# Attention stage: low parts of weights by subtraction on VectorE, or by an adding transfer from memory with the weights sent one ahead

## The chip, the cores and the metric

The kernel runs on one core of a Trainium2 chip. TensorE (PE) multiplies; VectorE (DVE) and ScalarE (ACT) do elementwise work; GpSimd (POOL) and SyncE (SP) mostly issue transfers (DMAs), each from a queue of its own that it works off in order. What counts is the device time of one execution in microseconds (us), the median of the runs.

## The reference

Two layers over 512 frames of width 1024, with 256 memory tokens. Layer 0 mixes by an RWKV-7 recurrence; layer 1, which the change touches, by attention to chunks. In short form:

```python
k_s, v_s = split(rms_norm(x, ln_kv) @ w_kv, 2)            # 12 heads of 64
h = rms_norm(x, ln1[1]);  p = h @ b_w_in                  # 768 mixer + 256 memory columns
s = q . k / 8 + rel_bias                                  # own chunk of 64 and 8 chunks before
mix = softmax(s) @ v
mo  = memory_attention(p[768:], mem_n, w_mem_kv[1])       # 4 heads, 256 memory tokens
x = x + concat([mix, mo]) @ w_out[1]
x = x + conv_glu(rms_norm(x, ln2[1]), ffn_in[1], ...)     # then a last rms_norm
```

All is float32.

## The kernel before, in words

**Three products for one.** A float32 matrix product is made of three products in a faster format (fp32r). Each operand is split into a high part (the value rounded to the format) and a low part (what is left), and PE adds high·high, high·low and low·high. `r1h`/`r1l` and `r2h`/`r2l` are the parts of the two normalised activations (`r1` for keys and values, `r2` for queries); `whi` and `wlo` are those of a weight of 128 x 1024 numbers, 512 KB.

**A weight's way to PE.** `load_w` has SP send the raw weight into `wraw` (L180; 2 buffers). `split_w` has ACT round it to `whi` (L169). Then the low part is made in one of two ways. By subtraction: DVE computes `wlo = wraw - whi` (L175). By an adding transfer: ACT writes the rounded negative, `wlo = -wraw` (L172), and POOL's queue sends the same weight from memory again, added onto it (L173). `whi` and `wlo` have 3 buffers each, so the low part of a weight can only be begun when PE is done with the low part of the third weight before it. The switch `lo_on` chooses; in the kernel before it is on only in layer 0's mixing stage.

**`dense`** multiplies one weight: 16 matmuls with the high part (L198, L199), then 8 with the low part (L202), each 512 columns wide. Its results lie in a PSUM tile `psd`, of which there are two.

**The attention stage** (from 782 us of the profiled execution) has 22 such weights: 6 for queries and 2 for memory queries (`wB`, `q_proj`), 6 for keys (`w_kvk`, `k_proj`), 3 times 2 for values (`w_kvv`, `v_proj`), and 2 of the output projection (`w_out`, `out_ahead`). `v_proj` makes a group of values, 256 columns, for 512 frames in four quarters; in a quarter each of 8 steps has three matmuls, two high (L1032, L1033) and one low (L1034), 256 wide; ACT then moves the quarter out (L1036, `vS`). The stage opens with `run(chain(*qk(0), v_proj(0)))`: q0, k0, then the first values. Then `weave` (L82) takes turns, by costs written beside each `yield`, between six pairs of attention heads with the memory attention (scores L1053/L1054, DVE L1058, exponentials on ACT L1060, DVE L1062, transposes L1068, copies on ACT L1070, products with values L1082) and the other projections. `attention` also loads the bias tiles `big` on SP (L1043) and has POOL write a corner of each (L1044).

A scheduler then fixes the order of every engine's instructions at build time; each engine works its own list off in order, so an instruction that waits holds up all that stands behind it on its engine.

Of the kernel before, what the change touches and what calls it, by code (L numbers as in the profile page):

```python
# [111 lines left out]
def trunk_kernel(ctx, tc, A, out):  # L112
# [25 lines left out]
    def Vc(name, i):  # L138
        return vec[:, VOFF[name][0] + i:VOFF[name][0] + i + 1]

    def ps_d(shape=(P, S)):
        return banks["D"].tile(list(shape), F32, name="psd", tag="psd")
# [17 lines left out]
    def tmp(dt=F32, shape=(P, S)):  # L160
        return banks["tmp"].tile(list(shape), dt, name="tmp", tag="tmp")


    lo_on = [0]

    def split_w(raw, n, src=None):
        hi = wp.tile([P, 1024], F32R, name="whi", tag="whi")
        lo = wp.tile([P, 1024], F32R, name="wlo", tag="wlo")
        SC.copy(hi[:, :n], raw)  # L169
        if src is not None:  # L170

            SC.activation(lo[:, :n], raw, AF.Copy, scale=-1.0)  # L172
            GP.dma_start(lo[:, :n], src, accum_op=ALU.add)  # L173
        else:
            V.tensor_tensor(lo[:, :n], raw, hi[:, :n], op=ALU.subtract)  # L175
        return hi, lo

    def load_w(src, n=1024):
        raw = wp.tile([P, 1024], F32, name="wraw", tag="wraw", bufs=2)
        nc.sync.dma_start(raw[:, :n], src)  # L180
        return split_w(raw[:, :n], n, src if lo_on[0] else None)
# [8 lines left out]
    def dense(ps, units, act, order=None, start=True, stop=True):  # L190

        ks = [(w, j, k) for w, kk in units for j, k in enumerate(kk)]
        if order is not None:
            ks = [next(q for q in ks if q[2] == k) for k in order]

        for n, ((wh, wl), j, k) in enumerate(ks):
            ah, al = act(k)
            PE.matmul(ps, wh[:, j * P:(j + 1) * P], ah, start=start and n == 0, stop=False)  # L198
            PE.matmul(ps, wh[:, j * P:(j + 1) * P], al, start=False, stop=False)  # L199
            yield 432  # L200
        for n, ((wh, wl), j, k) in enumerate(ks):
            PE.matmul(ps, wl[:, j * P:(j + 1) * P], act(k)[0], start=False, stop=stop and n == len(ks) - 1)  # L202
            if n % 2 or n == len(ks) - 1:
                yield 432 if n % 2 else 216
# [5 lines left out]
    def pair_of(h_, l_):  # L210
        return lambda k: (h_[:, k], l_[:, k])
# [25 lines left out]
    def scaled_split(src, m, gain, h_, l_):  # L237
        SC.activation(h_[:, m], src, AF.Copy, scale=Vc(gain, m))
        V.scalar_tensor_tensor(l_[:, m], src, Vc(gain, m), h_[:, m], op0=ALU.mult, op1=ALU.subtract)
# [73 lines left out]
        return 2 * (2 * (2 * score + 2 * 430) + 1720)  # L313


    def out_ahead(l, act, order, n, pre):

        for m in range(n):
            w = load_w(A["w_out"][l, m])
            ps = ps_d()  # L320
            pre.append((w, ps))
            yield from dense(ps[:], [(w, K8)], act, order=order, stop=False)
# [572 lines left out]
    pre = []  # L895
    lo_on[0] = 1
    for st_ in range(NPAIR + 1):
# [28 lines left out]
        if st_ == NPAIR:  # L926
            if NM < 18:
                gens.append((mA, mem_cost(860) * (18 - NM) / 18))
            gens.append((out_ahead(0, act1, [0, 1, 2, 3, 4] if NM < 18 else [0, 1, 2, 3, 6, 7, 4], 2, pre), (10 if NM < 18 else 14) * 648))
# [10 lines left out]
    act2 = pair_of(r2h, r2l)  # L940
# [11 lines left out]
    with ExitStack() as bctx:  # L952
# [15 lines left out]
        def take_back(*ms):  # L968
            for m in ms:
                yield lambda: (m if m < 4 else f"m{m - 6}") in done  # L970
                t_ = tmp()
                nc.sync.dma_start(t_[:], mixb[m])
                split_to(r2h[:, m], r2l[:, m], t_[:])
                yield 1

        for m in range(KD):
            scaled_split(xT[:, m], m, "ln_kv", r1h, r1l)


        done = set()  # L980
# [3 lines left out]
        def after_unit(i, n):  # L984
            at = UNITS.index(i) - n
            return lambda: at < 0 or UNITS[at] in done

        def q_proj(i, T, unit=None):
            yield after_unit(i if unit is None else unit, 3)
            w = load_w(A["wB"][i])  # L990
            ps = ps_d()
            yield from dense(ps[:], [(w, K8)], act2)
            q = tmp()
            V.scalar_tensor_tensor(q[:], ps[:], 0.125, rho[:], op0=ALU.mult, op1=ALU.mult)

            qs = ap_.tile([P, 2, S], F32R, name="qs", tag="qs", bufs=3)
            for h in range(2):
                SC.copy(qs[HS[h], h], q[HS[h]])
                V.tensor_tensor(qs[HS[1 - h], h], q[HS[h]], qs[HS[h], h], op=ALU.subtract)
            T["q"] = qs  # L1000

        def k_proj(i, T):
            yield after_unit(i, 2)
            w = load_w(A["w_kvk"][i])
            ps = ps_d()
            yield from dense(ps[:], [(w, K8)], act1)
            k_ = tmp()
            V.tensor_tensor(k_[:], ps[:], rho[:], op=ALU.mult)
            ks = ap_.tile([P, 2, S], F32R, name="ks", tag="ks")
            kl = ap_.tile([P, 2, S], F32R, name="kl", tag="kl")  # L1010
            for h in range(2):
                SC.copy(ks[HS[h], h], k_[HS[h]])
                SC.copy(ks[HS[1 - h], h], k_[HS[h]])
                for rows_ in HS:
                    V.tensor_tensor(kl[rows_, h], k_[HS[h]], ks[HS[h], h], op=ALU.subtract)
            T["k"] = ks, kl
# [3 lines left out]
        def v_proj(g):  # L1020
            yield lambda: g < 2 or 2 * g - 3 in done
            vS[g] = ap_.tile([P, 4, 256], F32, name="vS", tag="vS")
            wv = [load_w(A["w_kvv"][g, u]) for u in range(2)]
            for t2 in range(2):
                pp_ = ps_d()
                for t in (2 * t2, 2 * t2 + 1):
                    pt = pp_[:, (t % 2) * 256:(t % 2) * 256 + 256]
                    ts = slice(t * P, (t + 1) * P)
                    for k in range(8):
                        wh, wl = wv[k // 4]  # L1030
                        ws = slice((k % 4) * 256, (k % 4 + 1) * 256)
                        PE.matmul(pt, r1h[:, k, ts], wh[:, ws], start=k == 0, stop=False)  # L1032
                        PE.matmul(pt, r1l[:, k, ts], wh[:, ws], start=False, stop=False)  # L1033
                        PE.matmul(pt, r1h[:, k, ts], wl[:, ws], start=False, stop=k == 7)  # L1034
                        yield 324
                    SC.activation(vS[g][:, t], pt, AF.Copy, scale=rc[:, t:t + 1])  # L1036

        def attention(i, T):
# [54 lines left out]

        Tb = [{} for _ in range(NPAIR)]
        qk = lambda i: [q_proj(i, Tb[i]), k_proj(i, Tb[i])]
        run(chain(*qk(0), v_proj(0)))
        ptB = {}

# [7 lines left out]
        def mem_qk(f):  # L1106
            yield from q_proj(6 + f, Tm[f], f"m{f}")
            yield after_unit(f"m{f}", 2)
            ks = ap_.tile([P, 2, S], F32R, name="ks", tag="ks")
            kl = ap_.tile([P, 2, S], F32R, name="kl", tag="kl")  # L1110
            for h in range(2):
                SC.copy(ks[HS[h], h, :NMEM], kmT1[HS[h], f])
                SC.copy(ks[HS[1 - h], h, :NMEM], kmT1[HS[h], f])
                for rows_ in HS:
                    V.tensor_tensor(kl[rows_, h, :NMEM], kmT1[HS[h], f], ks[HS[h], h, :NMEM], op=ALU.subtract)
            Tm[f]["k"] = ks, kl
# [10 lines left out]
        def wait_for(c):  # L1127
# [4 lines left out]
        pre = []  # L1132
        att = [attention(i, Tb[i]) for i in range(NPAIR)]
        weave([(chain(*att[:2], wait_for(lambda: "k" in Tm[1]), memB, *att[2:]), NPAIR * ATT_COST + mem_cost(430)),
               (chain(*qk(1), mem_qk(0), mem_qk(1), v_proj(1), *qk(2), *qk(3), v_proj(2), q_proj(4, Tb[4]),
                      q_proj(5, Tb[5]), k_proj(4, Tb[4]), take_back(0, 1, 2, 6, 7), k_proj(5, Tb[5]), take_back(3),
                      out_ahead(1, act2, [0, 1, 2, 6, 7, 3], 2, pre)),
                1.05 * (6 * 16 * 648 + 2 * 32 * 324 + 12 * 648))])

    with ExitStack() as fctx:  # L1140
        open_banks(fctx, S=2, F=4)
# [123 lines left out]
```

## Time and profile before

| | |
|---|---|
| median of 3 runs | 1388.37 us (1387.73 to 1388.55) |
| profiled execution | 1385.81 us, of which 1384.0 us from the first to the last instruction |
| busy in it | PE 96%, DVE 60%, ACT 44%, POOL 2% |
| attention stage | about 782 to 976 us; output projection to 1012; channel mixer to the end |

Rows of the profile read as follows. A group or timeline row names the line, the engine, the operation and "out<-in" tiles; an arrow "<-" in brackets, or at a row's end, names what ended the idle time before the instruction. A waits row says who waited, at which line, for which engine and line, for how long in total, how many times, and the longest.

### The profile page before, as it was taken

To read this page: it belongs to the slowest core of one execution; us is meant where nothing else is said; L and a number is where in the kernel's file an instruction comes from. 1 tells how busy PE (TensorE), PEld (TensorE's weight loads), DVE (VectorE), ACT (ScalarE), POOL (GpSimd) and SP (SyncE) were. 2 spreads that over 40 slices of the span, in tenths; PEclk is the share of its full clock that TensorE was granted. 3 is DMA by queue.
4 is the path that set the end of the run, shared out by engine and by line. 5 is a ranking of instruction groups with operands and counts; after the bars stand their busy time and mean duration, and the time that the engine had idled before them with its cause. 6 is when DMAs were issued, how large, how long until landed. Compare 5 with 4: busy or idle time off the path is not lost. (4 is left out here: it accounts for less than half of the span.)

```text
span 1384.0 us, 20864 instructions
## 1 busy us (share of the span) xinstructions
PE 1331.9 (96%) x8266; PEld 1075.5 (78%) x8266; DVE 826.1 (60%) x1752; ACT 612.7 (44%) x1022; POOL 33.7 (2%) x55
## 2 busy tenths in 40 slices
PE   6999999998899999999999999999999999999996
PEld 4877777775678888888888887787788888888886
DVE  7876789776356565655343567658566555553324
ACT  6556556544344333333232466657443333332321
POOL 3000000000000000000000000000000000000000
PEclk9999999998789999999999999999999999999998
DMA  5275544460042223233233331233222322322332
GB/s 180 87 214 128 110 108 106 94 159 24 1 152 92 91 94 104 92 99 95 73 110 98 124 107 65 93 106 99 92 92 91 105 94 93 106 88 82 104 95 74
DMA packets 63506, 139.18 MB, mean 101 GB/s; under 512 B 24624, under 2 KB 28336, under 8 KB 63408
## 3 DMA queue, kind: packets, MB, share of 16 engines
q1 hardware_dynamic: 60672, 127.89, 29.4%
q0 software_dynamic: 2736, 9.96, 4.3%
q8 instruction: 65, 1.06, 0.3%
q14 instruction: 33, 0.27, 0.1%
HBM read 131.01 MB, written 6.82 MB: 100 GB/s over the span
## 5 line engine op out<-in xcount | busy, mean ns | idle before, releaser
L175 DVE TENSOR_TENSOR wlo<-wraw,whi 128x1024 fp32r<-128x1024 f32 x183 | 218.9, 1197 | 130.1 <-PE psd L202 119.9
L169 ACT CAST whi<-wraw 128x1024 fp32r<-128x1024 f32 (+1 forms) x202 | 207.8, 1030 | 156.5 <-DMA wraw<-in_ffn_out_dram 40.5
L198 PE MATMUL psd<-r1h,whi 128*128 128x512 f32 x336 | 138.9, 414 | 5.4 <-ACT r1h L214 3.8
L198 PE MATMUL psf<-r1h,whi 128*128 128x512 f32 x352 | 137.2, 390 | 0.0
L198 PE MATMUL psf<-r2h,whi 128*128 128x512 f32 x352 | 137.1, 390 | 0.0
L199 PE MATMUL psf<-r1l,whi 128*128 128x512 f32 x352 | 137.0, 389 | 0.0
L199 PE MATMUL psf<-r2l,whi 128*128 128x512 f32 x352 | 137.0, 389 | 0.0
L199 PE MATMUL psd<-r1l,whi 128*128 128x512 f32 x336 | 135.1, 402 | 0.0
L202 PE MATMUL psd<-r1h,wlo 128*128 128x512 f32 x336 | 95.5, 411 | 3.1 <-DMA wlo<-in_wA_dram 3.1
L199 PE MATMUL psd<-f3l,whi 128*128 128x512 f32 (+1 forms) x238 | 88.6, 377 | 0.0
L198 PE MATMUL psd<-f3h,whi 128*128 128x512 f32 (+1 forms) x238 | 88.5, 376 | 0.0
L202 PE MATMUL psf<-r1h,wlo 128*128 128x512 f32 x352 | 87.0, 389 | 0.0
L202 PE MATMUL psf<-r2h,wlo 128*128 128x512 f32 x352 | 86.9, 389 | 0.0
L358 DVE TENSOR_TENSOR tmp<-psf,rho 128x512 f32<-128x512 f32 x44 | 30.4, 692 | 94.7 <-PE psf L202 94.7
L198 PEld LDWEIGHTS psd<-r1h,whi 128*128 128x128 f32 x336 | 64.4, 192 | 22.0 <-ACT r1h L214 4.2
L198 PE MATMUL psd<-r2h,whi 128*128 128x512 f32 (+1 forms) x200 | 77.5, 391 | 0.1
L199 PE MATMUL psd<-r2l,whi 128*128 128x512 f32 (+1 forms) x200 | 76.3, 384 | 0.8 <-DVE r2l L215 0.8
L202 PEld LDWEIGHTS psf<-r1h,wlo 128*128 128x128 f32 x352 | 66.1, 188 | 13.7
L202 PEld LDWEIGHTS psf<-r2h,wlo 128*128 128x128 f32 x352 | 66.1, 188 | 13.7
L198 PEld LDWEIGHTS psf<-r1h,whi 128*128 128x128 f32 x352 | 66.1, 188 | 13.7
L199 PEld LDWEIGHTS psf<-r1l,whi 128*128 128x128 f32 x352 | 66.1, 188 | 13.7
L198 PEld LDWEIGHTS psf<-r2h,whi 128*128 128x128 f32 x352 | 66.1, 188 | 13.7
(324 smaller groups left out, 2433.1 us busy)
## 6 DMA issues: line engine op xcount, KB each, us to landing
wraw<-in_ffn_in_dram SPq DMA_DIRECT2D x88, 512.0 KB, 3.3
wraw<-in_ffn_out_dram SPq DMA_DIRECT2D x32, 448.0 KB, 3.3
wraw<-in_wA_dram SPq DMA_DIRECT2D x20, 512.0 KB, 3.9
wlo<-in_wA_dram POOLq DMA_DIRECT2D x17, 512.0 KB, 7.9
wraw<-in_w_out_dram SPq DMA_DIRECT2D x16, 512.0 KB, 3.7
wraw<-in_ffn_out_dram SPq DMA_DIRECT2D x16, 512.0 KB, 4.4
wraw<-in_wB_dram SPq DMA_DIRECT2D x8, 512.0 KB, 3.4
Lr<-d SPq DMA_DIRECT2D x24, 128.0 KB, 5.6
```

The lines of the kernel that those rows point to most:

```text
L169: SC.copy(hi[:, :n], raw)
L175: V.tensor_tensor(lo[:, :n], raw, hi[:, :n], op=ALU.subtract)
L198: PE.matmul(ps, wh[:, j * P:(j + 1) * P], ah, start=start and n == 0, stop=False)
L199: PE.matmul(ps, wh[:, j * P:(j + 1) * P], al, start=False, stop=False)
L202: PE.matmul(ps, wl[:, j * P:(j + 1) * P], act(k)[0], start=False, stop=stop and n == len(ks) - 1)
L358: V.tensor_tensor(v[:], pv[:], rho[:], op=ALU.mult)
```

## The change

`lo_on` is set from the split of the key/value norm to the end of the weave, so all 22 weights of the attention stage get their low parts by the adding transfer. `take_w` hands out the weights from one written list, and keeps two sent: when a weight is taken, the next is already on its way. In `v_proj` the 16 high matmuls of a quarter stand first and the 8 low ones after them. The number of matmuls is the same.

```diff
@@ attention stage, before the projections
             scaled_split(xT[:, m], m, "ln_kv", r1h, r1l)
+        lo_on[0] = 1
...
+        order_ = [("q", 0), ("k", 0), ("v", 0), ("q", 1), ("k", 1), ("q", 6), ("q", 7), ("v", 1), ("q", 2), ("k", 2),
+                  ("q", 3), ("k", 3), ("v", 2), ("q", 4), ("q", 5), ("k", 4), ("k", 5), ("o", 0), ("o", 1)]
...
+        def take_w(_=None):
+            while srcs and len(sent) < 2:
+                sent.append(load_w(srcs.pop(0)))
+            return sent.pop(0)
@@ q_proj, k_proj (v_proj and out_ahead alike)
-            w = load_w(A["wB"][i])
+            w = take_w()
@@ v_proj
                         PE.matmul(pt, r1h[:, k, ts], wh[:, ws], start=k == 0, stop=False)
                         PE.matmul(pt, r1l[:, k, ts], wh[:, ws], start=False, stop=False)
+                        if k % 2:
+                            yield 432
+                    for k in range(8):
+                        wh, wl = wv[k // 4]
+                        ws = slice((k % 4) * 256, (k % 4 + 1) * 256)
                         PE.matmul(pt, r1h[:, k, ts], wl[:, ws], start=False, stop=k == 7)
-                        yield 324
+                        if k % 4 == 3:
+                            yield 432
...
+        lo_on[0] = 0
```

The lists move at the opening of the stage. PE's list there, before: the first `psd` is q0 (`r2h`, `r2l`), the second k0 (`r1h`, `r1l`), and `pss` holds the sums of the norm.

```order
L199 MATMUL psd<-r2l,whi 128x512
L244 MATMUL pss<-cst,acc 128x2 x4
L198 MATMUL psd<-r2h,whi 128x512
L198 MATMUL psd<-r1h,whi 128x512
L199 MATMUL psd<-r1l,whi 128x512
L199 MATMUL psd<-r2l,whi 128x512
L202 MATMUL psd<-r2h,wlo 128x512 x8
L198 MATMUL psd<-r1h,whi 128x512
```

And PE's list at the same place after:

```order
L244 MATMUL pss<-cst,acc 128x2 x4
L199 MATMUL psd<-r2l,whi 128x512
L198 MATMUL psd<-r2h,whi 128x512
L198 MATMUL psd<-r1h,whi 128x512
L199 MATMUL psd<-r2l,whi 128x512
L199 MATMUL psd<-r1l,whi 128x512
L198 MATMUL psd<-r1h,whi 128x512
L202 MATMUL psd<-r2h,wlo 128x512 x8
L199 MATMUL psd<-r1l,whi 128x512
```

Three matmuls of k0 instead of two now stand ahead of q0's eight low ones (L202); all else of k0 still stands behind them.

ACT's list at the opening, before (`L238` splits the norm's activations, `L255` moves the norm's factor `rho` out, `L998` starts on q0's result):

```order
L169 CAST whi<-wraw 128x1024 x2
L238 ACTIVATE r1h<-xT,vec 128x512 x7
L231 ACTIVATE tmp<-xT 128x512
L238 ACTIVATE r2h<-xT,vec 128x512
L238 ACTIVATE r1h<-xT,vec 128x512
L169 CAST whi<-wraw 128x1024 x2
L255 COPY rho<-pss 128x512
L169 CAST whi<-wraw 128x1024
```

And after:

```order
L169 CAST whi<-wraw 128x1024 x2
L238 ACTIVATE r1h<-xT,vec 128x512 x7
L172 ACTIVATE wlo<-wraw 128x1024 x2
L231 ACTIVATE tmp<-xT 128x512
L238 ACTIVATE r2h<-xT,vec 128x512
L238 ACTIVATE r1h<-xT,vec 128x512
L169 CAST whi<-wraw 128x1024
L172 ACTIVATE wlo<-wraw 128x1024
L169 CAST whi<-wraw 128x1024
L172 ACTIVATE wlo<-wraw 128x1024
L255 COPY rho<-pss 128x512
```

The negatives of q0 and k0 (first L172 row) come behind the seven activations `r1h`; those of the two halves of the first values (v0) follow, and the second half's is the fourth low part of the stage, so it goes into the buffer of q0's and waits for q0's eight low matmuls on PE.

More of the change, by code (lines that the diff above doesn't have):

```diff
@@ L313, in mem_cost, with out_ahead @@
         return 2 * (2 * (2 * score + 2 * 430) + 1720)
-    def out_ahead(l, act, order, n, pre):
+    def out_ahead(l, act, order, n, pre, load=load_w):
         for m in range(n):
-            w = load_w(A["w_out"][l, m])
+            w = load(A["w_out"][l, m])
             ps = ps_d()
@@ L986, in after_unit @@
             return lambda: at < 0 or UNITS[at] in done
+        order_ = [("q", 0), ("k", 0), ("v", 0), ("q", 1), ("k", 1), ("q", 6), ("q", 7), ("v", 1), ("q", 2), ("k", 2),
+                  ("q", 3), ("k", 3), ("v", 2), ("q", 4), ("q", 5), ("k", 4), ("k", 5), ("o", 0), ("o", 1)]
+        srcs = []
+        for n_, i_ in order_:
+            srcs += ([A["w_kvv"][i_, u] for u in range(2)] if n_ == "v" else
+                     [{"q": A["wB"], "k": A["w_kvk"], "o": A["w_out"][1]}[n_][i_]])
+        sent = []
+        def take_w(_=None):
+            while srcs and len(sent) < 2:
+                sent.append(load_w(srcs.pop(0)))
+            return sent.pop(0)
         def q_proj(i, T, unit=None):
             yield after_unit(i if unit is None else unit, 3)
-            w = load_w(A["wB"][i])
+            w = take_w()
             ps = ps_d()
@@ L1003, in k_proj @@
             yield after_unit(i, 2)
-            w = load_w(A["w_kvk"][i])
+            w = take_w()
             ps = ps_d()
@@ L1022, in v_proj @@
             vS[g] = ap_.tile([P, 4, 256], F32, name="vS", tag="vS")
-            wv = [load_w(A["w_kvv"][g, u]) for u in range(2)]
+            wv = [take_w() for u in range(2)]
             for t2 in range(2):
@@ L1136, in trunk_kernel @@
                       q_proj(5, Tb[5]), k_proj(4, Tb[4]), take_back(0, 1, 2, 6, 7), k_proj(5, Tb[5]), take_back(3),
-                      out_ahead(1, act2, [0, 1, 2, 6, 7, 3], 2, pre)),
+                      out_ahead(1, act2, [0, 1, 2, 6, 7, 3], 2, pre, take_w)),
                 1.05 * (6 * 16 * 648 + 2 * 32 * 324 + 12 * 648))])
+        lo_on[0] = 0
     with ExitStack() as fctx:
```

## The prediction

> **What bounds the kernel now.** I read the page's first row, then the stretches of the attention stage beside the stage that already uses adding transfers, then PE's waits.
>
> ```profile
> PE 1331.9 (96%) x8266; PEld 1075.5 (78%) x8266; DVE 826.1 (60%) x1752; ACT 612.7 (44%) x1022; POOL 33.7 (2%) x55
> ...
> core 0: us, PE busy (x) PEld busy (x) DVE busy (x) ACT busy (x) POOL busy (x), PEclk, DMA share, GB/s
> 782.00:985.00 203.00, 199.02 (x1118) 156.68 (x1117) 137.46 (x347) 129.75 (x293) 1.95 (x12) 1.00 0.30 100
> 110.00:300.00 190.00, 184.15 (x2309) 140.31 (x2311) 149.27 (x511) 110.20 (x201) 12.08 (x14) 1.00 0.50 109
> 782.00:800.00 18.00, 17.00 (x96) 14.17 (x94) 15.48 (x31) 9.57 (x14) 0.43 (x3) 1.00 0.66 208
> ```
>
> PE bounds it. In the attention stage (782 to 985) it is busy 199.02 of 203.00 us at the full clock, so 4.0 us are idle: nothing that only relieves other engines can gain more there. DVE is busy 137.46 us (68%). These are all of PE's waits between 780 and 990:
>
> ```profile
> PE psd L199 <- DVE r2l L215: 0.8, 1, 0.8
> PE psd L1032 <- ACT vS L1036: 0.6, 1, 0.6
> PE pss L1068 <- DVE sb L1062: 0.6, 3, 0.2
> PE pss L1082 <- ACT ptT L1070: 0.5, 2, 0.3
> PE pss L1054 <- DVE kl L1015: 0.3, 1, 0.3
> PE psd L1032 <- DVE tmp L994: 0.3, 1, 0.3
> ```
>
> Together 3.1 us, of which DVE's rows have 0.8 + 0.6 + 0.3 + 0.3 = 2.0. No matmul waits for a low part now.
>
> **The change part by part.** Subtractions go, negatives and adding transfers come; their prices stand in the stage's group of L175 and in layer 0's rows of L172 and L173:
>
> ```profile
> L175 DVE TENSOR_TENSOR wlo<-wraw,whi 128x1024 fp32r<-128x1024 f32 x26 | 31.7, 1220 | 2.7 <-ACT whi L169 2.6
> ...
> L172 ACT ACTIVATE wlo<-wraw x19: 1053/1061/1087, 86.6 to 299.8; 128x1024 fp32r<-128x1024 f32 x19
> ...
> L173 POOL DMA_DIRECT2D wlo<-in_wA_dram x17: 862/862/1011, 88.0 to 276.4; - x17
> ...
> DMA to landing us min/median/max: 5.2/7.9/8.6
> ```
>
> DVE loses 22 x 1.22 = 26.8 us, ACT gains 22 x 1.06 = 23.3 us (129.75 becomes 153 of 203), POOL 22 x 0.86 = 19 us. None of it is PE's work; it counts only where PE waits. What counts is the delay of one low part: by subtraction 1.22 us behind the cast; by transfer 1.06 (L172), then some 0.33 until POOL starts (87.98 less 87.65 in the rows below), then 7.9 from issue to landing (5.2 to 8.6): **9.3 us from the negative's start to a usable low part, 6.6 to 10.0**. Layer 0's first one shows it whole:
>
> ```profile
> 86.59 1.06 ACT L172 ACTIVATE wlo<-wraw 128x1024 fp32r<-128x1024 f32 x1
> 87.98 1.01 POOL L173 DMA_DIRECT2D wlo<-in_wA_dram  x1 [51.39 <-DVE Xu L666]
> 95.96 1.22 PE L202 MATMUL psd<-r1h,wlo 128*128 128x512 f32 x2 [3.06 <-DMA wlo<-in_wA_dram]
> ```
>
> 95.96 - 86.59 = 9.4 us, and PE waited 3.06 us for it. The other 18 transfers of that stage cost PE no wait, at a DMA share of 0.50. So I expect trouble at the opening and little later. The opening now:
>
> ```profile
> 777.39 4.41 ACT L238 ACTIVATE r1h<-xT,vec 128x512 fp32r<-128x512 f32 x7 [1.94 <-PE psd L202]
> 783.51 0.63 ACT L231 ACTIVATE tmp<-xT 128x512 f32<-128x512 f32 x1 [1.71 <-DVE xT L370]
> 784.68 4.17 SPq L180 DMA_DIRECT2D wraw<-in_w_kvv_dram  x2
> 787.26 1.98 PE L202 MATMUL psd<-r2h,wlo 128*128 128x512 f32 x8
> 792.70 2.00 PE L202 MATMUL psd<-r1h,wlo 128*128 128x512 f32 x8
> 794.98 0.39 PE L1032 MATMUL psd<-whi,r1h 128*128 128x256 f32 x1 [0.28 <-DVE tmp L994]
> 795.20 0.28 PE L1033 MATMUL psd<-whi,r1l 128*128 128x256 f32 x1
> 795.32 0.28 PE L1034 MATMUL psd<-wlo,r1h 128*128 128x256 f32 x1
> 799.43 0.47 ACT L1036 ACTIVATE vS<-psd,rc 128x256 f32<-128x256 f32 x1
> 799.96 0.39 PE L1032 MATMUL psd<-whi,r1h 128*128 128x256 f32 x1 [0.64 <-ACT vS L1036]
> ```
>
> 1. **q0's low part: +3.5.** ACT can start its negative only behind the seven L238, at 777.39 + 4.41 = 781.80; it is usable at 781.8 + 9.3 = 791.1. PE wants it at 787.26, or 787.5 with the one more matmul of k0 that now stands ahead (1.98 / 8 = 0.25). PE's list is in order and the rest of k0 stands behind the eight, so it waits 791.0 - 787.5 = 3.5 us; with the ends, 6.6 and 10.0, +0.9 to +4.3. I take the median because the first case of layer 0 agrees with it.
> The two negatives fill ACT to 783.9, past 783.51 where L231 starts now; the 0.4 us by which the last r2h comes later lies under this wait, and would be paid if the wait were gone.
> 2. **k0's low part: 0.** Its negative ends at 783.9, POOL starts behind q0's issue at about 784.3, and it lands at 792.2; PE wants it at 792.70 + 3.5. Were the first wait gone, it would be wanted at 792.70 and late by at most 0.2 (8.6 instead of 7.9).
> 3. **v0's second half: +1.7.** Its buffer is q0's, so its negative starts when q0's low matmuls end, 791.0 + 2.0 = 793.0, and it lands at 802.3. PE starts v0 at 794.98 - 0.28 + 3.5 = 798.2, and 16 high and 4 low matmuls at 0.12 us (795.32 - 795.20) bring it to 800.6. 802.3 - 800.6 = +1.7; with the ends 0 and +2.5. The first half has a free buffer: raw sent about 783, cast at 787 to 788, landing near 798, wanted at 800.1, so 0. Had the low matmuls stayed between the high ones, the second half would be wanted after 12 matmuls and not 20, and the wait would be 1.0 longer: that is what the new order of the value products is worth.
> 4. **Waits that go: -0.9.** The 0.28 and the 0.64 in the last rows: k0's and q0's results are moved out while PE waits, and seven matmuls of the next PSUM tile now stand where PE waited for vS. Ends 0 and -0.9.
> 5. **DVE relieved later: -0.9.** DVE's other waits are 0.8 + 0.6 + 0.3 = 1.7; they end in chains through ACT and PE too, and ACT gets the work, so I take half. Ends 0 and -1.7.
> 6. **ACT's load: 0**, covered by its idle 203 - 153 = 50 us; ends 0 and +1.5, by the ACT rows of PE's waits (0.6 + 0.5) and some more if they repeat.
> 7. **The later transfers: 0, up to +2.** The tightest is v2's second half, which takes q3's buffer (its predecessors are k3 and v2's first half):
>
> ```profile
> 889.96 0.62 PE L202 MATMUL psd<-r2h,wlo 128*128 128x512 f32 x2
> ...
> 898.86 0.36 PE L1032 MATMUL psd<-whi,r1h 128*128 128x256 f32 x1
> ```
>
> From 890.6 it may begin, and it is wanted 20 matmuls after 898.86, at 901.3: 10.7 us for 9.3, spare 1.4. v1's second half has some more, keys and queries over 4. POOL's other work there, the corners of `big`, shares the in-order queue with the transfers:
>
> ```profile
> POOL big L1044 <- DVE st L1061: 23.0, 2, 20.5
> ```
>
> A corner that waits so for its buffer holds back the low parts behind it; in the list before nothing stood behind it. In layer 0's stage POOL had no such work between its transfers, so that this is a difference to my precedent; I leave it to the rival below. The weights that are sent one ahead come sooner on SP's queue, and two of the first three `big` loads later by two weight loads; no matmul waits for `big` now (the rows of PE's waits name none), so 0.
>
> Sum: 3.5 + 1.7 - 0.9 - 0.9 = **+3.4 us**, 1389.2 for an execution like the profiled one (1385.81, itself 2.6 below the median shown). Against the median: 1388.37 + 3.4 = **1391.8 us**.
>
> **The rivals.**
>
> *Transfers as quick as plain loads; DVE the hidden limit (faster).* A plain load of the same size lands sooner:
>
> ```profile
> wlo<-in_wA_dram POOLq DMA_DIRECT2D x17, 512.0 KB, 7.9
> ...
> wraw<-in_wB_dram SPq DMA_DIRECT2D x8, 512.0 KB, 3.4
> ```
>
> With 3.4 for 7.9, q0's low part is there at 781.8 + 1.4 + 3.4 = 786.6, ahead of 787.5, v0's half too: terms 1 and 3 are nothing and 1388.37 - 0.9 - 0.9 = 1386.6 remains, no change that can be told. It decides from a landing of 787.5 - 781.8 - 1.4 = 4.3 us, and the shortest of 17 took 5.2. [...] Chance 0.06. If besides DVE's queue was behind all of PE's idle time (against it: DVE's named waits are 2.0 of the 4.0), the whole 4.0 us go: 1384.4, faster. For it stands that DVE is busy 15.48 of the opening's 18.00 us. Chance 0.10.
>
> *Transfers late all along (slower by more).* The opening already has a DMA share of 0.66, layer 0's stage 0.50; 22 x 512 KB more, or a corner of `big` ahead, could make 12 us of the 9.3. Then q0 costs 6.2, v0's second half 791.0 + 2.7 + 2.0 + 12 = 807.7 against 803.3, so 4.4, v2's half 12 - 10.7 = 1.3; with -1.8 that is +10.1: 1398.5. Against it, layer 0's 18 transfers without a wait. [...] Chance 0.16.
>
> **How the numbers follow.** About 0.2%, 2.8 us, is what a measurement of this kernel can tell from no change: faster is below 1385.6, slower above 1391.1. My forecast has 0.68; its ends are +0.9 + 0 - 2.6 = -1.7 (1386.7) and +4.3 + 2.5 + 0 + 1.5 = +8.3 (1396.7). The centre lies just above the bound, so of the 0.68 I give 0.42 to slower, 0.25 to the same and 0.01 to faster. With the rivals: slower 0.42 + 0.16 = 0.58, same 0.25 + 0.06 = 0.31, faster 0.11. The range 1386.5 to 1396.7 leaves out the faster rival (0.10) and most of the late one.
>
> **What would show it.** In the changed profile PE waits for "DMA wlo<-in_wB_dram" at L202 for 3 to 4 us near 787 to 791 (term 1), for "DMA wlo<-in_w_kvv_dram" at the low matmuls of v0 for 1 to 2 us near 801 (term 3), and nowhere else for a low part (term 7); the waits for DVE's tmp and ACT's vS are gone there (term 4), DVE's others shorter (term 5). L175 falls from 183 to 161, L172 rises from 19 to 41. I would be wrong by a landing under 5.2 us or over 10 at the opening, or by a low part awaited at each weight.

## The result, and the profile after

The changed kernel takes 1400.74 us (median of 4 runs, 1398.82 to 1402.51) against 1388.05 us of the kernel before beside it: a ratio of 1.0093, 95% interval 1.0075 to 1.0110, some 12.7 us more. The sign was forecast; the size, +3.4 us and a range up to 1396.7, was not.

The profiled execution took 1402.51 us, span 1400.7. The page's first row, then the stretch of the attention stage and four parts of its opening, and all of PE's waits there (780 to 1000 us); columns as before.

```profile
PE 1338.7 (96%) x8266; PEld 1080.8 (77%) x8266; DVE 803.1 (57%) x1730; ACT 631.3 (45%) x1044; POOL 52.4 (4%) x77
...
782.00:985.00 203.00, 188.06 (x1052) 150.34 (x1051) 106.01 (x314) 140.95 (x304) 21.12 (x34) 0.97 0.60 151
...
788.00:792.90 4.90, 0.92 (x4) 0.40 (x3) 2.32 (x13) 2.00 (x2) 0.86 (x1) 0.99 1.03 253
793.00:796.00 3.00, 3.00 (x7) 2.42 (x8) 0.00 (x0) 1.05 (x1) 0.00 (x0) 0.50 1.06 236
797.00:800.00 3.00, 3.00 (x17) 2.55 (x16) 1.14 (x2) 2.22 (x4) 0.00 (x0) 1.00 1.04 336
...
807.00:810.00 3.00, 2.99 (x14) 2.99 (x15) 0.50 (x1) 0.47 (x1) 0.00 (x0) 0.52 1.00 218
```

```profile
PE pss L1103 <- ACT ptT L1091: 4.7, 4, 3.2
PE psd L202 <- DMA wlo<-in_wB_dram: 4.0, 1, 4.0
PE psd L1054 <- DMA wlo<-in_w_kvv_dram: 2.8, 1, 2.8
PE pss L1089 <- DVE sb L1083: 2.7, 5, 1.2
PE pss L1074 <- ACT ks L1028: 0.3, 2, 0.2
PE psd L198 <- DVE tmp L1023: 0.2, 1, 0.2
```

PE's idle time in the stage went from 4.0 to 203.00 - 188.06 = 14.9 us. The waits are 14.7 in all, where they were 3.1. But PE is also busy 6.8 us longer over the span (1338.7 for 1331.9) with the same 8266 matmuls. The rows of the opening show a part of the reason: behind the first wait, from 793 to 796, and behind the second, from 807 to 810, PE's clock is granted at half (0.50 and 0.52). The timeline of PE shows what that does to q0's eight low matmuls, 1.98 us before:

```profile
792.97 3.61 PE L202 MATMUL psd<-r2h,wlo 128*128 128x512 f32 x8 [4.05 <-DMA wlo<-in_wB_dram]
```

From the start times of single matmuls in the timeline, in us:

| from, to | before | after | more |
|---|---|---|---|
| start of the execution to q0's first matmul | 782.0 | 783.3 | 1.3 |
| q0's first matmul to the first score | 22.7 | 31.3 | 8.6 |
| first score to the last score | 161.1 | 167.8 | 6.7 |
| last score to the end | 418.3 | 418.3 | 0.0 |

The first row is not the change's: layer 0's recurrence there takes another time in each execution (q0 began at 779.3 to 785.7 over the profiles that leave layer 0 as it was). The stage itself takes 15.3 us longer in this execution, which is the slowest of the four: 8.6 at the opening and 6.7 later.

### The profile page after: what moved, and what is told of

It is laid out like the page before. It is cut to its first block, busy times and chain, and to the rows that moved or that the text cites. A ratio compares the mean times of both kernels' runs of the same rounds, so it can differ in the third digit from the quotient of the medians.

```text
span 1400.7 us, 20908 instructions
## 1 busy us (share of the span) xinstructions
PE 1338.7 (96%) x8266; PEld 1080.8 (77%) x8266; DVE 803.1 (57%) x1730; ACT 631.3 (45%) x1044; POOL 52.4 (4%) x77
## 3 DMA queue, kind: packets, MB, share of 16 engines
q8 instruction: 65, 1.06, 0.3%
## 4 chain that ended last, share of the span: by engine, by line
PE 77%; DVE 9%; ACT 5%; DMA 4%; issue 3%; SPq 0%; DVEq 0%; POOL 0%; ACTq 0%; POOLq 0%
PE psf L199 11%; PE psf L198 11%; PE psf L202 11%; PE psd L198 10%; PE psd L199 10%; PE psd L202 10%; PE pss L1103 1%; DVE Xu L666 1%; DMA big<-in_rel_dram 1%; DVE sb L1079 1%; PE pss L795 1%; DVE Xs L668 1%; PE pss L286 1%; PE pss L807 1%; PE psl L827 1%
## 5 line engine op out<-in xcount | busy, mean ns | idle before, releaser
L175 DVE TENSOR_TENSOR wlo<-wraw,whi 128x1024 fp32r<-128x1024 f32 (+1 forms) x161 | 192.2, 1194 | 127.7 <-PE psd L202 120.5
L202 PE MATMUL psd<-r1h,wlo 128*128 128x512 f32 x336 | 94.5, 407 | 2.9 <-DMA wlo<-in_wA_dram 2.9
L202 PE MATMUL psf<-r1h,wlo 128*128 128x512 f32 x352 | 87.0, 389 | 0.0
L202 PE MATMUL psf<-r2h,wlo 128*128 128x512 f32 x352 | 86.9, 389 | 0.0
L199 PEld LDWEIGHTS psf<-r2l,whi 128*128 128x128 f32 x352 | 66.2, 188 | 13.7
L202 PEld LDWEIGHTS psf<-r1h,wlo 128*128 128x128 f32 x352 | 66.1, 188 | 13.8
L202 PEld LDWEIGHTS psf<-r2h,wlo 128*128 128x128 f32 x352 | 66.1, 188 | 13.7
```

## Experiments

The theory T that the runs tested has three parts: the opening waits for low parts; PE's clock falls to half behind the long waits (those of 2.81, 3.15 and 4.05 us in the changed kernel each came with 3.4 us at 0.50); and later in the stage the adding transfers delay the plain loads (weight loads landed in a median of 5.1 us, 3.5 before), which ACT's in-order list hands on to the exponentials. All ratios are to the kernel before on the same chip, with 95% intervals.

**The new order of the value products alone.** Only the part of the diff in `v_proj`:

```diff
                         PE.matmul(pt, r1l[:, k, ts], wh[:, ws], start=False, stop=False)
+                        if k % 2:
+                            yield 432
+                    for k in range(8):
+                        wh, wl = wv[k // 4]
+                        ws = slice((k % 4) * 256, (k % 4 + 1) * 256)
                         PE.matmul(pt, r1h[:, k, ts], wl[:, ws], start=False, stop=k == 7)
-                        yield 324
+                        if k % 4 == 3:
+                            yield 432
```

> The kernel before with only the new order of the value products (16 high, then 8 low). Theory T (the 12 us are waits for low parts and loads that the adding transfers delay, each followed by a lower granted clock): no change, within 3 us of before, no PE wait over 1.5 us in the attention stage. Rival R2 (the new order of the value products, which also shifts the turns of the weave, costs the time of the later waits): at least 3 us slower than before, with the wait of the value products for the copies of the transposes (3.2 us at 935 to 939 in the changed kernel) there too.

Measured: 1.0000 (0.9988 to 1.0013); the longest PE wait in the stage is 1.3 us, for vS. R2 falls: the order costs nothing, and brings nothing either.

**One ahead, by subtraction.**

```diff
-        lo_on[0] = 1
+        lo_on[0] = 0
```

> The changed kernel with all low parts by subtraction again (one ahead and the new order stay). Theory T: within 3 us of before (1385 to 1391), no PE wait over 1.5 us, weight loads land in 3 to 4 us. Rival R1 (sending one ahead makes loads and casts hold up SP's and ACT's queues, so bias tiles and transposes come late, whatever way the low part is made): 4 us or more slower than before, with the 3.2 us wait near 935 still there.

Measured: 0.9999 (0.9986 to 1.0013), and no PE wait above 0.9 us. Weight loads in the stage land in 3.1 to 4.8 us, 3.3 in the middle. R1 falls: sending one ahead is harmless. So the loss needs the adding transfers.

**The first four by subtraction.** `lo_on` is set only from q1 on.

```diff
             while srcs and len(sent) < 2:
+                lo_on[0] = int(len(srcs) <= 18)
                 sent.append(load_w(srcs.pop(0)))
```

> The changed kernel with the first four weights (q0, k0, both halves of v0) by subtraction and the other 18 by adding transfers. Theory T: the two opening waits (4.0 and 2.8 us) and the clock lost after them (0.78 and 0.66 in two stretches of 5 us, some 3 us of work) go, so 8 to 10 us less than the changed kernel: 2 to 5 us slower than before, from the 3.2 us wait near 935 and the waits for the last pair. If the opening waits alone were the cost and the clock played no part: 6 to 7 us less. Rival R1: 3 us or less is won, as the waits reappear with the next weights.

Measured: 1.0017 (1.0006 to 1.0028), 2.3 us above before, so about 10 us of the 12.7 are gone. The opening takes 22.9 us, as before (22.7). What is left is between the scores: 164.8 us for 161.1 in the profiled execution, which is slower than the median of this run.

**Not one ahead.**

```diff
-            while srcs and len(sent) < 2:
+            while srcs and len(sent) < 1:
```

> The changed kernel with each weight sent when it is taken, not one ahead; all by adding transfers. Theory T: the opening wait for q0 stays (about 4 us), the second half of v0 waits at least as long, and low parts come late at several later weights as well, so 10 to 20 us slower than before. Rival R1 (the loads sent ahead are what holds the queues): clearly faster than the changed kernel, 6 us or less above before.

Measured: 1.0073 (1.0058 to 1.0088), 10 us above before, T's lower end and far from R1's. PE waits 4.5 us for q0's low part and 2.2 for v0's. The low parts that T saw late "at several later weights as well" are not: there is no third wait for one, and this part of T falls. Sending the weights ahead shows no worth beside adding transfers: the interval here overlaps that of the changed kernel (1.0075 to 1.0110).

**Dummy matmuls where PE runs dry.** This run separates the wait from the clock.

```diff
+        for n in range(fill):
+            PE.matmul(ps, ks[0][0][0][:, 0:P], act(0)[0], start=True, stop=True)
...
-            yield from dense(ps[:], [(w, K8)], act2)
+            yield from dense(ps[:], [(w, K8)], act2, fill=26 if i == 0 else 0)
...
+                    if g == 0 and t == 0:
+                        for n in range(8):
+                            PE.matmul(pt, r1h[:, 0, ts], wv[0][0][:, 0:256], start=True, stop=True)
```

> The changed kernel with 34 dummy matmuls on PE where it would otherwise run dry: 26 of 512 columns ahead of q0's first product and 8 of 256 ahead of v0's, 26 x 0.25 + 8 x 0.12 = 7.4 us of work that the output doesn't need (the real products overwrite it). The time from the first matmul of q0 to the first score was 22.7 us before (1.7 of them idle) and 31.3 in the changed kernel. Theory T (after a wait of 3 us or more PE's clock is granted low for some us, which is part of the 8.6): the granted clock stays at 1.00 in this stretch, which takes 21.0 + 7.4 = 28.4 us and what waits are left (0 to 1.5): 28 to 30, so 1.5 to 3 us less than the changed kernel although PE does more. Rival (the clock's figure tells nothing, the waits or other slowness are the whole loss): 31 us or more.

Measured: 1.0072 (1.0053 to 1.0091). The opening takes 30.0 us, so the rival (31 or more) falls. PE's busy time from q0's first matmul to the first score, in the kernel before, the changed kernel and this run, and the one wait that is left here:

```profile
781.95:804.62 22.67, 21.67 (x134) 18.84 (x132) 16.71 (x32) 10.05 (x15) 0.43 (x3) 1.00 0.54 174
```

```profile
783.26:814.60 31.34, 24.46 (x133) 21.20 (x132) 11.26 (x27) 14.62 (x20) 4.74 (x8) 0.89 0.82 210
```

```profile
784.46:814.50 30.04, 28.52 (x167) 24.78 (x166) 11.25 (x27) 14.64 (x20) 4.75 (x8) 1.00 0.85 219
...
PE psd L1059 <- DMA wlo<-in_w_kvv_dram: 1.5, 1, 1.5
```

The expectation took 1.7 us of idle time for the kernel before; the row has 22.67 - 21.67 = 1.0. In the changed kernel PE is idle 6.9 us, 5.9 more, and busy 2.8 us longer with the same products. It worked there through 6.2 us at half clock (792.97 to 796.25 and 807.01 to 809.90), which is 3.1 us of lost work and so about what the 2.8 are. In this run the clock stays at 1.00, through a wait of 1.5 us too; the idle time is 1.5 us, and the other 6.9 us of busy time are the dummies. PE does 6.9 us of useless work, and the opening is still 1.3 us shorter. So of the 8.6 us that the opening lost, some 5.9 are waiting and 2.8 are the half clock.

**ACT's extra work without the transfers.** The negatives are written, then overwritten by the subtraction.

```diff
             SC.activation(lo[:, :n], raw, AF.Copy, scale=-1.0)
-            GP.dma_start(lo[:, :n], src, accum_op=ALU.add)
+            if lo_on[0] == 2:
+                V.tensor_tensor(lo[:, :n], raw, hi[:, :n], op=ALU.subtract)
+            else:
+                GP.dma_start(lo[:, :n], src, accum_op=ALU.add)
...
-        lo_on[0] = 1
+        lo_on[0] = 2
```

> The changed kernel in which ACT writes the 22 negatives as well (L172), but the low part is then made by subtraction on DVE over them, and nothing is sent a second time. It has ACT's extra 23 us without the extra transfers. Theory T (the later loss comes from plain loads that land late beside adding transfers, so that ACT's casts and splits hold up the exponentials and copies behind them): within 3 us of before, no PE wait over 1.5 us between 830 and 990. Rival R3 (the negatives on ACT's in-order list alone delay the exponentials and copies): 3 to 6 us slower than before, with the waits for the transposes at 945 to 975 there too.

Measured: 0.9999 (0.9983 to 1.0015). R3 falls: ACT is busy 146.33 us of 203 in the stage and nothing that shows is lost.

**Only the middle twelve by adding transfers.**

```diff
+                lo_on[0] = int(6 < len(srcs) <= 18)
```

> Adding transfers for the 12 weights in the middle alone (from q1 to v2's second half); the first four and the last six (q4, q5, k4, k5 and two of the output projection) by subtraction. Theory T: the later loss lies in the tail, where the adding transfers meet the loads that bring the parked heads back (L972), so within 2 us of before. Rival R4 (every adding transfer costs its share, 2.3 us for 18 of them): 1.5 us slower.

Measured: 0.9994 (0.9982 to 1.0007). Twelve adding transfers cost nothing that shows, and gain nothing that shows.

**Only the last six.**

```diff
+                lo_on[0] = int(len(srcs) <= 6)
```

> Adding transfers for the last six weights alone, the other 16 by subtraction. Theory T: the whole later loss, as in the run with the first four by subtraction: 2 to 4 us slower than before, with PE's waits for the transposes (DVE sb) at 945 to 975 and a granted clock under 1.00 there. Rival R4: 0.8 us slower (6 of 18 shares).

Measured: 1.0028 (1.0015 to 1.0042), 3.9 us, against 2.3 for 18 of them with these six among them: R4's shares fall, the later loss is the tail's. It can be followed there. First the loads that bring the parked heads back (source view of L972, before and then this run), then its timeline and the stretch behind:

```profile
DMA to landing us min/median/max: 2.9/3.6/4.6
```

```profile
  ACT r2h L214: 1.8, 2
...
DMA to landing us min/median/max: 2.8/5.2/7.7
```

```profile
948.35 0.62 ACT L214 CAST r2h<-tmp 128x512 fp32r<-128x512 f32 x1 [0.91 <-DMA tmp<-mixb]
...
949.83 0.62 ACT L214 CAST r2h<-tmp 128x512 fp32r<-128x512 f32 x1 [0.86 <-DMA tmp<-mixb]
...
950.36 0.61 ACT L1082 ACTIVATE sb<-sb,st 128x384 f32<-128x384 f32 x1
...
951.10 0.16 DVE L1083 RECIPROCAL st<-st 128x1 f32<-128x1 f32 x1 [2.14 <-ACT sb L1082]
...
952.23 0.55 PE L1090 MATMUL pss<-cst,sb 128*128 128x128 f32 x3 [2.06 <-DVE sb L1084]
```

```profile
952.97:956.38 3.41, 3.26 (x11) 1.85 (x10) 3.41 (x9) 3.25 (x8) 0.14 (x1) 0.50 0.44 154
```

The parked head lands late; ACT's split of it (L214) stands ahead of the exponential (L1082); DVE and then PE's transposes wait, 2.06 us; then the clock is at 0.50 for 3.4 us. The 2.1 us of waiting and half of the 3.4 us make the 3.8 by which the stretch between the scores is longer here (164.9).

**The first two of layer 0.** Layer 0's first adding transfer had shown the same: the row with the wait of 3.06 us, quoted ahead of the result, is followed in the kernel before by this stretch:

```profile
95.96:101.00 5.04, 5.04 (x23) 3.78 (x24) 2.01 (x7) 1.04 (x1) 0.59 (x1) 0.50 1.01 250
```

Five us at half clock. So the kernel before pays at its own opening the price that the change adds at the second.

The diff is of the first of two runs; in the second, `skip` is 2.

```diff
+    skip = [1]
...
-        return split_w(raw[:, :n], n, src if lo_on[0] else None)
+        late = lo_on[0] and skip[0] <= 0
+        skip[0] -= lo_on[0]
+        return split_w(raw[:, :n], n, src if late else None)
```

> The kernel before, with one difference in layer 0's mixing stage: its first weight with an adding transfer (PE waited 3.06 us for it at 95.96, and its clock was granted at 0.50 from there to 101) gets its low part by subtraction. Theory T (an opening weight by adding transfer costs its wait and some 1.7 to 2.5 us of half clock): 3 to 5 us faster than before, unless the second weight's transfer (landing at 100.4) is then waited for in its place. Rival (DVE is busy with a chain there, 8 to 9 tenths of each us, so that the subtraction delays that chain instead): no change within 2 us.

Measured: 0.9980 (0.9967 to 0.9994), 2.8 us faster (0.8 to 4.6), a little under T's 3 to 5. The rival (no change within 2 us) lies in the interval too, so this run alone does not settle it.

> As the run before this one, with the first two weights of layer 0's adding transfers by subtraction. Theory T: 3 to 6 us faster than before, no PE wait for a low part over 1 us and no granted clock of 0.50 between 90 and 105. Rival (DVE's chain): no change or slower, with PE waiting for DVE there.

Measured: 0.9968 (0.9950 to 0.9986), 4.4 us faster, so the rival falls. The stretch from 90 to 105 us has its full clock:

```profile
90.00:95.00 5.00, 5.00 (x34) 3.95 (x33) 4.79 (x14) 4.35 (x7) 0.03 (x1) 1.00 0.55 186
95.00:100.00 5.00, 4.61 (x21) 3.47 (x19) 4.76 (x16) 3.79 (x5) 1.77 (x2) 1.00 0.93 210
100.00:105.00 5.00, 3.52 (x94) 3.29 (x95) 3.71 (x26) 3.26 (x6) 0.08 (x1) 1.00 0.98 245
```

Somewhat later in this profile the clock is low where the kernel before had it in full (from 115 to 125 us, before and this run):

```profile
115.00:125.00 10.00, 9.59 (x105) 7.01 (x105) 7.48 (x14) 7.63 (x15) 0.86 (x1) 1.00 0.87 194
```

```profile
115.00:125.00 10.00, 9.52 (x89) 7.41 (x88) 5.14 (x9) 4.74 (x9) 0.55 (x1) 0.66 0.79 177
```

The low clock begins at 116.4, and no wait of PE over 0.6 us stands in the 10 us ahead of that; what let the clock fall there is not shown. So not all of the half clock is won back.

**Both together**: these two by subtraction, and in the attention stage adding transfers for the middle twelve alone.

> The two put together: layer 0's first two adding weights by subtraction, and in the attention stage adding transfers for the 12 weights in the middle alone. Theory T: the gain of the run before this one and no more, as the attention stage's middle gave 0.8 us within its uncertainty: 3 to 6 us faster than before.

Measured: 0.9940 (0.9921 to 0.9959), 8.3 us faster, the best of all. That is more than T said; the sum of the two parts, 4.4 + 0.8, lies below its interval of 5.7 to 11, though with the parts' own intervals it can be met. Whether the middle twelve add something of their own here stays open, since the stage between the scores is only 1.0 us shorter in the profile (160.1) and layer 0's time varies most.

**q0 and k0 alone by subtraction.**

```diff
+                lo_on[0] = int(len(srcs) <= 20)
```

> The changed kernel with q0 and k0 alone by subtraction. Theory T: q0's wait (4.0 us and its clock) is gone; v0's second half still takes q0's buffer, from 789.3 on, lands 9.3 us later at 798.6 and is wanted at 797.1: a wait near 1.5 us, too short for the clock to fall (a 1.5 us wait left it at 1.00 in the run with dummy matmuls). So q0 to the first score takes 22.7 + 1 to 2 us, 0 to 2 us more than with the first four by subtraction, and 3 to 6 us above before in all. If the opening's second wait were as bad by itself as in the changed kernel (2.8 us and half clock): 4 to 5 us more than with the first four.

Measured: 1.0056 (1.0043 to 1.0068), 7.8 us above before; the opening takes 27.7 us, 5.0 more than before. This expectation missed: it looked at v0's second half, and the first one came too late. The rows of that half, and the stretch behind:

```profile
792.55 1.05 ACT L172 ACTIVATE wlo<-wraw 128x1024 fp32r<-128x1024 f32 x1
...
793.90 0.86 POOL L173 DMA_DIRECT2D wlo<-in_w_kvv_dram  x1 [4.25 <-ACT wlo L172]
...
801.99 0.74 PE L1055 MATMUL psd<-wlo,r1h 128*128 128x256 f32 x4 [2.65 <-DMA wlo<-in_w_kvv_dram]
```

```profile
802.00:809.00 7.00, 6.35 (x33) 6.05 (x34) 0.33 (x1) 0.96 (x2) 0.86 (x1) 0.60 1.02 258
```

The raw load of that half waits for a `wraw` buffer that DVE frees with q0's subtraction, so the negative starts only at 792.55; 801.99 is 9.4 us later, the chain that the prediction had, and 2.65 us too late for PE. The clock fell again, to 0.60 over these 7 us. A half that is begun late is enough.

## Why the prediction was wrong

The waits at the opening were right in place and kind. Two steps failed: a wait was priced at its length alone, without the half clock behind it (2.8 us), and the later transfers were put at nothing (2.3 to 3.9 us by the runs). Point by point:

- **Term 1, q0's low part (+3.5).** PE waited 4.05 us, since this transfer landed 8.6 us after its issue and not 7.9. Close. What was not in the term is the clock: 3.61 us instead of 1.98 for the eight low matmuls, 1.6 more. This is the first step that failed: the price of a wait was set equal to its length. The evidence was in the trace of before: the precedent of 3.06 us was quoted, and the granted clock behind it was not asked for.
- **Term 2, k0 (0).** Right: no wait for it.
- **Term 3, v0's second half (+1.7).** It waited 2.8 us, and the clock fell again. The chain had one more link than the term. POOL's timeline in the changed kernel, and PE's row:

```profile
796.53 0.14 POOL L1065 MEMSET big<- 64x64 f32 x1 [5.13 <-DMA big<-in_rel_dram]
801.07 0.14 POOL L1065 MEMSET big<- 64x64 f32 x1 [4.39 <-DMA big<-in_rel_dram]
801.56 0.86 POOL L173 DMA_DIRECT2D wlo<-in_w_kvv_dram  x1 [0.35 <-issue]
807.01 1.22 PE L1054 MATMUL psd<-wlo,r1h 128*128 128x256 f32 x4 [2.81 <-DMA wlo<-in_w_kvv_dram]
```

ACT had the negative done at 797.7, right behind q0's low matmuls as the term had it. But a corner of `big` stood ahead on POOL and waited for its load until 801.07. That is the late rival's "corner of `big` ahead", which got its chance and no place in the sum. What it cost is not separated from the load on the transfer engines at that time (a DMA share of 0.96 from 797 to 807) by any run.

- **Term 4, waits that go at the opening (-0.9).** Right in the sum: the waits for tmp (0.28) and vS (0.64) do not show in the changed kernel's opening. But this goes with the longer waits there: with the new order and no wait for a low part, PE waited 1.3 us for vS (the order alone).
- **Term 5, DVE relieved later (-0.9).** Not seen. The later waits grew (the table of waits above), and twelve subtractions less on DVE gave 0.9994, nothing that can be told.
- **Term 6, ACT's load (0).** Right, shown by the run with ACT's work alone.
- **Term 7, the later transfers (0, up to +2).** No low part was late after v0, as said. But beside the transfers others came late, which the term did not price, and this is the second step that failed: the loads of SP's queue. (The upper end of the range also left out the term's own +2; with it, it would have been 1398.7.) Landing times of the weight loads in the stage (source view of L180, 782 to 985 us), before and after:

```profile
DMA to landing us min/median/max: 3.1/3.5/4.8
```

```profile
DMA to landing us min/median/max: 3.1/5.1/11.8
```

In the profiled execution one of these made the third long wait, k4's weight (issued at 929.21, among two adding transfers at 929.07 and 931.25):

```profile
937.18 1.04 ACT L169 CAST whi<-wraw 128x1024 fp32r<-128x1024 f32 x1 [4.71 <-DMA wraw<-in_w_kvk_dram]
938.14 1.06 ACT L1091 COPY ptT<-pss 128x512 f32<-128x512 f32 x2
...
938.77 0.64 PE L1103 MATMUL pss<-ptT,vS 128*64 128x512 f32 x1 [3.15 <-ACT ptT L1091]
```

```profile
940.00:943.00 3.00, 3.00 (x13) 1.84 (x10) 1.37 (x2) 1.27 (x3) 0.92 (x2) 0.50 0.78 253
```

ACT's list has the cast of the late weight ahead of two copies that PE needs, and the clock is at half behind the wait. Term 6 looked at ACT's idle 50 us; what cost time was not ACT's load but what its next instruction waited for. In two other runs with all 22 adding transfers (not ahead, dummy matmuls) this wait did not form and the stretch between the scores was 1.7 to 1.8 us longer, not 6.7; the tail's waits stayed. So the profiled execution, the slowest of the four timed, may show more of it than the others.

**The rivals.** "Transfers as quick as plain loads" did not come: 5.3 to 10.9 us from issue to landing. "Late all along" came nearest in time, 1398.5 for 1400.74, for a mixed reason: the low parts were not late all along, as this rival had it, but plain loads beside the transfers were, and the corner of `big` held POOL's queue as it said. The half clock was not in it either. The forecast's range ended below it.

Summed again with what the runs showed: opening 4.0 + 2.8 (waits) - 0.9 (term 4) + 2.8 (clock) = 8.7, for 8.6 in the profile; tail 2.3 to 3.9, by the runs with the first four by subtraction and with the last six alone; together 11.0 to 12.6, for 12.7 measured.

## What to carry to other kernels

A wait of PE cost more than it lasted here: price a new wait of the lengths seen in these traces (2.06 to 4.05 us) with the half clock behind it (at the least 3.4 us at 0.50, of which PE worked through 2.9 to 3.4, so 1.4 to 1.7 us of lost work), and look for that clock behind the waits that the kernel already has, where part of it can be won back. An adding transfer has to be begun early: in four cases where PE waited for one, 9.4 to 10.4 us went by from the start of the negative to the first matmul with the low part (86.59 to 95.96 in layer 0 before, 783.01 to 792.97 and 796.62 to 807.01 in the changed kernel, 792.55 to 801.99 with q0 and k0 by subtraction), while in the run with the middle twelve alone PE waited for none of them and nothing was lost that shows (0.9994). At the opening here q0's negative was begun at 783.0 for a use at 788.9, and the subtraction was the better choice; whether the negative could be begun sooner, no run tries. And a slower transfer was paid here by the loads beside it (weight loads landed in a median of 5.1 us for 3.5) and by what stood behind their consumers in ACT's in-order list (waits of PE of 2.06 and 3.15 us), so ask of a "free" engine what its next instruction waits for, not how busy it is.

## What the runs showed of the hardware

- **The clock behind a pause.** Pauses of PE of 2.06, 2.65, 2.81, 3.06, 3.15 and 4.05 us were each followed by, or ended in, a stretch at a granted clock of 0.50, of 3.4 us, or twice that behind those of 2.65 (803.34 to 810.17) and 3.06 (95.56 to 102.39); a pause of 1.5 us in the run with dummy matmuls was not. The length of one pause is not all: in the run with the first four by subtraction, waits of 0.5 to 1.2 us a few us apart had the clock at half behind them too.

```profile
956.66 0.55 PE L1090 MATMUL pss<-cst,sb 128*128 128x128 f32 x3 [1.22 <-DVE sb L1084]
```

```profile
958.40:961.80 3.40, 3.40 (x11) 2.62 (x12) 3.40 (x8) 2.51 (x7) 0.14 (x1) 0.50 0.46 147
```

  The clock came back after such a stretch: in the changed kernel it stood at 0.50 from 793 to 796 and at 1.00 from 797 to 800, with PE busy all through.
- **What an adding transfer takes.** The rows of the DMA queues in the changed kernel, plain loads first and then POOL's adding ones (packets, MB, share of 16 engines):

```profile
q1 hardware_dynamic: 60672, 127.89, 28.7%
q0 software_dynamic: 5904, 21.50, 8.8%
```

Per MB that is 0.22% for the plain queue, with loads of all sizes, and 0.41% for the adding one: 1.8 times the time of the transfer engines per byte. In the opening of the attention stage the DMA share stood at 1.03 to 1.06 from 788 to 800 (the rows of the opening above; the share passes 1 there), and at 1.01 behind layer 0's first wait. So by this share these engines were full there, which the share of 0.50 over all of layer 0's stage had hidden.
